# Two-block transformer step: adaptive shift and scale by PE products, division after the weighted sum, gate work one expert pair earlier

## The chip, the cores and the metric
One NeuronCore of one Trainium2 chip runs the whole program. The metric is device microseconds of one execution. TensorE (PE), VectorE (DVE), ScalarE (ACT) and GpSimd (POOL) each run their own instructions in order; SyncE (SP) issues most transfers, ACT and POOL a few.

## The reference, cut to what matters
```python
def first_block(x, c, ...):
    c_act = jax.nn.silu(c)
    mod = c_act @ ada_w[l] + ada_b[l]
    sh_a, sc_a, gt_a, sh_m, sc_m, gt_m = [m[:, None, :] for m in jnp.split(mod, 6, axis=-1)]
    h = rmsnorm(x, norm_mix_g[l]) * (1.0 + sc_a) + sh_a
    proj = h @ w_in[l]                      # four mixers of 4 heads
    x = x + gt_a * (mixed @ w_out[l])
    h = rmsnorm(x, norm_ffn_g[l]) * (1.0 + sc_m) + sh_m
    x = x + gt_m * conv_ffn(h, ...)

def forgetting_attention(...):              # one of the four mixers
    s = q @ k * scale + (cq[..., :, None] - cum[..., None, :])
    p = jax.nn.softmax(jnp.where(dist >= 0, s, NEG), axis=-1)
    return p @ v

def second_block(x, p, ...):
    x = x + jnp.concatenate([y_pool, y_attn], axis=-1) @ w_out[i]
    x = x + expert_choice_ffn(rms_norm(x, norm_ffn[i]), ...)      # 16 experts
    g = jax.nn.sigmoid(rms_norm(x, norm_ple[i]) @ w_ple_gate[i])
    e = rms_norm(p[i] @ w_ple_proj[i], norm_ple_post[i])
    x = x + g * e
```
x is 512 tokens of 1024 features in float32, c one vector of 1024. An expert has 1024 x 2048 gate and up weights and 2048 x 1024 down weights and takes 64 tokens. Subtracting the query's own term cq from a row of scores does not change that row's softmax, and dividing a row of exponentials by its sum can be done before or after the product with v.

## The kernel before, in words
Activations of the first block and of the second block's attention lie with features on the partitions: eight blocks of 128 features by 512 tokens. A product in float32 precision is made of three fp32r products (`mm3`, lines 331 to 334) of a high and a low half; `weights_` (lines 318 to 326) splits a weight panel on ACT (`whi`) and DVE (`wlo`). A scheduler orders the instructions of each engine from the program and its priorities; on the chip each engine keeps that order.

**Start (lines 264 to 504).** x is loaded in four pieces, then the shift and scale columns of ada_w, transposed, as eight 1 MB tiles `adr` in a ring of four (`ada_load`, line 299). `bd` and `tb2` (lines 458, 461) are a round trip through memory that makes the bias table; the products `pf` (line 511) reverse it with the matrix `flip`, a part of `cst` that line 505 loads. The eight squares of x are summed, `rstd_rows` and `to_features` make the reciprocal root `rr` for each token, and x is multiplied by it (line 481, half on DVE and half on POOL). For each feature block k, DVE reduces the shift's half of `adr` against c (line 485), POOL multiplies the scale's half (line 490) and ACT sums it (line 491); DVE makes `shf` and `amul`, and ACT and DVE make `hTh` and `hTl` (lines 495 to 497). The first three projections (`early`) run along, block by block.

**Mixers (to line 1050).** Four mixers in two halves each run two at a time as generators; `run` mixes them with the projections that come next. `ada_more` (line 348) computes the other four vectors of mod out of 64 tiles `adw` of 256 KB with two buffers: POOL multiplies a tile by its element of c (line 355) and adds it to `ada_a` (line 360); after eight tiles four PE products `pm` sum over partitions. 48 of the tiles come during the mixers. `fox` (line 851) is the forgetting attention: for each of four query blocks and two heads, `fb` is the key's cumulative gate less the query's (line 861) plus the causal mask (line 862); `softmax_part` (line 613) adds it to the scores and takes the exponential, `scale_parts` (line 638) divides both heads' exponentials by their sums `l` (lines 639 and 643), then they are transposed and multiplied by v. `na` (line 1184), in the second block, has the same steps for eight heads, two at a time.

**Experts (line 1060 to the end).** Experts come in pairs. A pair reads 48 chunks of 1 MB (`chunk`, line 1294), each used by eight products with 64 output rows, the two experts' products side by side in PE's two column halves (lines 1697, 1698, 1727, 1728). Chunks lie in rings of buffers: 2 `x16`, 5 `chy`, 6 `chr`, 3 `chl`. `chl` is used for chunks until pair E_AT, `chr` until pair RETIRE; then they hold the embedding (`pe`), the gate's weights and its sums. Between the steps of a pair, `between` gives PACE turns to a list of other work: `spread` (an expert's output onto the tokens), `embedding`, `gate_base` (the gate's products `pg` of one block of 128 tokens, started in the pairs that BASE names) and `gate_pair` (the products `z` of a pair's own output with the gate's weights, and their scatter `po` onto the blocks whose base is done).

Of the kernel before, what the change touches and what calls it, by code (L numbers as in the profile page):

```python
# [9 lines left out]
FT = mybir.dt.float32  # L10
# [9 lines left out]
D = 1024  # L20
# [6 lines left out]
SCV = []  # L27
# [3 lines left out]
PACE = [1.0, 1.0, 1.0, 1.0, 2.2, 2.2, 2.2, 2.2]  # L31
# [5 lines left out]
RETIRE = 4  # L37
BASE = {4: [0], 5: [1], 6: [2], 7: [3]}
E_AT = 2
# [79 lines left out]
def prep(i):  # L119
# [33 lines left out]
    o["c"] = i["c"].reshape(1, D)  # L153
# [5 lines left out]
    aw = i["ada_w"][0][:, :2 * D].T.reshape(2, 8, 128, D)  # L159
    o["adaT"] = np.ascontiguousarray(aw.transpose(1, 2, 0, 3)).reshape(8, 128, 2 * D)  # L160
# [70 lines left out]
def _build(ctx, tc, nc, a, dbg, stop):  # L231
# [35 lines left out]
    cact = su.tile([128, D], FT, name="cact")  # L267
    A.dma_start(cact, bcast(a["c"], D))
# [30 lines left out]
    def ada_load(n):  # L299
        for j in range(n):  # L300
            t = su.tile([128, 2 * D], FT, name="adr", tag="adr", bufs=4)
            SY.dma_start(t, a["adaT"][len(ada_raw)])
            ada_raw.append(t)
# [45 lines left out]
    def ada_more(n):  # L349

        for m in range(ada_next[0], min(64, ada_next[0] + n)):
            w = tmp[0].tile([128, 512], FT, name="adw", tag="adw", bufs=2)
            SY.dma_start(w, a["ada2"][m])
            k = m % 8
            P.tensor_tensor(w, w, cT[:, k:k + 1].to_broadcast([128, 512]), op=OP.mult)  # L355
            if k == 0:
                ada_next[1] = tmp[0].tile([128, 512], FT, name="ada_a", tag="ada_a", bufs=1)
                P.tensor_copy(ada_next[1], w)
            else:
                P.tensor_tensor(ada_next[1], ada_next[1], w, op=OP.add)  # L360
            if k == 7:
                pm = ps("pm", "dense", 2)
                for j in range(4):
                    T.matmul(pm[:, j:j + 1], ada_next[1][:, 128 * j:128 * j + 128], K["ones"], start=True, stop=True)
                c_ = slice(16 + m // 8 * 4, 20 + m // 8 * 4)
                V.tensor_tensor(mod[:, c_], pm[:, 0:4], C["ada_b"][:, c_], op=OP.add)
            ada_next[0] = m + 1

    def rstd_of(acc, scale, out, n=128):

        v, y = sm([128, 8], "rv")[0:n, 0:out.shape[-1]], sm([128, 8], "ry")[0:n, 0:out.shape[-1]]
        V.tensor_scalar(v, acc, scale, EPS, op0=OP.mult, op1=OP.add)
        A.activation(y, v, AF.Ln)
        A.activation(y, y, AF.Exp, scale=-0.5)
        V.scalar_tensor_tensor(v, v, -0.5, y, op0=OP.mult, op1=OP.mult)
        V.tensor_tensor(v, v, y, op=OP.mult)
        V.scalar_tensor_tensor(out, v, 1.5, y, op0=OP.add, op1=OP.mult)

    def rstd_rows(sq, ind, n, scale, tag="dense"):

        ms = ps("ms", tag, 2)
        for t in range(4):
            T.matmul(ms[:, n * t:n * t + n], sq[:, 128 * t:128 * t + 128], ind, start=True, stop=True)
        y = sm([128, 16], "rs")[:, 0:4 * n]
        for c in range(0, 4 * n, 8):
            rstd_of(ms[:, c:min(c + 8, 4 * n)], scale, y[:, c:min(c + 8, 4 * n)])
        return y
# [64 lines left out]
    for k in range(8):  # L452
        ada_load(1)
        for e in range(2) if k == 0 else range(k + 1, k + 2):
            if e < EARLY:
                raws.append(panel(a["w_in"][e]))
        if k == 0:
            SY.dma_start(bd, bv)
        if k == TBK:
            for j in range(4):  # L460
                SY.dma_start(tb2[:, j].rearrange("p (h c) -> p h c", h=2),
                             bass.AP(tensor=bd.tensor, offset=bd.offset + 768 * j, ap=[[1, 128], [384, 2], [1, 256]]))
    sq = []
# [15 lines left out]
    shf = cp.tile([128, 8], FT, name="shf")  # L479
    for k in range(8):  # L480
        (V if k < XV else P).tensor_tensor(xin[:, k], xin[:, k], rr, op=OP.mult)
    for k in range(8):
        c_ = slice(k, k + 1)
        w = ada_raw[k]
        V.scalar_tensor_tensor(w[:, 0:D], w[:, 0:D], 1.0, cact, op0=OP.mult, op1=OP.mult, accum_out=mod[:, c_])
        sc = mod[:, 8 + k:9 + k]
        if k in SCV:
            V.scalar_tensor_tensor(w[:, D:], w[:, D:], 1.0, cact, op0=OP.mult, op1=OP.mult, accum_out=sc)
        else:
            P.tensor_tensor(w[:, D:], w[:, D:], cact, op=OP.mult)  # L490
# [153 lines left out]

    def pv(acc_, v, p_, i, sizes, start, stop):
# [78 lines left out]
    cqc = pa.tile([128, 16], FT, name="cqc")  # L724

    def gates_and_decay():
# [14 lines left out]
        V.tensor_copy(t[0:4], cum)  # L741
# [6 lines left out]
        V.tensor_copy(cqc.rearrange("p (t c) -> p t c", t=4), pg[:, :, 0:4])  # L748
# [102 lines left out]
    def fox(hp):  # L851
        q, kk, v, ckb = st["fox", hp]
        o = ps("od", "o", 2)
        for i in range(4):
            nk = 128 * (i + 1)
            l = sm([128, 2], "l2")
            e = []
            for par in range(2):
                h = 2 * hp + par
                fb = t2k("fb")  # L860
                V.tensor_scalar(fb[:, :nk], ckb[:, par, :nk], cqc[:, 4 * i + h:4 * i + h + 1], None, op0=OP.subtract)
                V.tensor_tensor(fb[:, nk - 128:nk], fb[:, nk - 128:nk], K["cm"], op=OP.add)
# [8 lines left out]
        A.activation(mix[:, 2 + hp], o, AF.Copy)  # L871
# [312 lines left out]
    def na(hp):  # L1184
        q, kk, v, nb = st["na", hp]
        o = ps("od", "o", 2)
        for b in range(4):
            nk = 248 if b else 256
            l = sm([128, 2], "l2")
            e = []  # L1190
            for par in range(2):
# [14 lines left out]
        m, o = mix2[:, 4 + hp].rearrange("p (r c) -> p c r", r=8), o.rearrange("p (c r) -> p c r", r=8)  # L1206
# [593 lines left out]
```

## Time and profile before
| what | value |
|---|---|
| median of 3 runs | 2106.22 us (2103.95 to 2110.03) |
| the profiled execution | 2106.01 us |
| its span, first to last instruction | 2104.2 us |
| mean granted TensorE clock | 0.972 of full speed |
| busy: PE, DVE, ACT, POOL | 1904.4, 851.3, 555.5, 243.8 us |
| moved by transfers | 523.67 MB |

Busy is the time in which an engine executes, stage by stage with different limits, so the shares of the whole span say little about any one stage. The page, the windows by stage, the chain of waits and the timeline are views of one execution. Ends of PE's products are modelled; what one product costs PE is read from the distance of starts.

### The profile page before, as it was taken

What the parts mean: (1) busy time and instruction counts of PE and PEld (TensorE: products, weight loads), DVE (VectorE), ACT (ScalarE), POOL (GpSimd) and SP (SyncE); (2) the same over time, 40 slices, a digit from 0 to 9 for tenths busy, and PEclk for the clock granted to TensorE, in tenths of its full rate; (3) what the DMA queues carried; (4) which work ended last, traced back from release to release, by engine and by line L of the source; (5) the groups of instructions that cost most, each with busy time, mean ns of one, the idle gap of its engine ahead of it and who ended that gap; (6) DMA issues with size and microseconds to landing.
All of it is one profiled execution on the core that took longest, in us unless ns stands there. A gap on an engine that the chain in (4) does not pass through costs nothing.

```text
span 2104.2 us, 22827 instructions
## 1 busy us (share of the span) xinstructions
PE 1904.4 (91%) x8822; PEld 1067.6 (51%) x8822; DVE 851.3 (40%) x1761; ACT 555.5 (26%) x1089; POOL 243.8 (12%) x211
## 2 busy tenths in 40 slices
PE   2898988979999999999989988988779999999997
PEld 1566656658888887777643322322223333333343
DVE  7887887875444335677441101210010020110114
ACT  4655544534323324445310000200000000100012
POOL 5540333350200000000100000000030000000001
PEclk9998998989999999999989999999989999999998
DMA  6532223333322223222589999899999999999991
GB/s 245 167 116 66 86 81 93 108 101 105 112 107 92 100 91 100 76 79 77 237 357 421 422 422 420 368 420 419 421 419 395 420 385 367 418 390 396 401 387 68
DMA packets 95084, 523.67 MB, mean 249 GB/s; under 512 B 11405, under 2 KB 12853, under 8 KB 44032
## 3 DMA queue, kind: packets, MB, share of 16 engines
q1 hardware_dynamic: 89936, 501.53, 60.9%
q0 software_dynamic: 3552, 17.82, 2.3%
q10 hardware_dynamic: 1488, 2.87, 0.4%
q8 instruction: 69, 1.13, 0.2%
q14 instruction: 39, 0.32, 0.0%
HBM read 510.83 MB, written 4.27 MB: 245 GB/s over the span
## 4 chain that ended last, share of the span: by engine, by line
PE 67%; DMA 18%; DVE 10%; ACT 2%; issue 2%; POOL 0%; SPq 0%; DVEq 0%; POOLq 0%; ACTq 0%
DMA ch<-in_w_ue_dram 8%; DMA ch<-in_w_de_dram 6%; PE ua L1697 5%; PE ga L1697 4%; PE ga L1698 4%; PE yd L1728 4%; PE yd L1727 3%; PE pg L1553 3%; PE z L1553 2%; PE ag L332 2%; PE ag L333 2%; PE ag L334 2%; PE od L649 2%; PE av L332 2%; PE av L333 2%; PE av L334 2%
## 5 line engine op out<-in xcount | busy, mean ns | idle before, releaser
L1697 PE MATMUL ga<-ch,xe 128*64 128x512 f32 x512 | 242.5, 610 | 9.0 <-DMA ch<-in_w_ge_dram 9.0
L1698 PE MATMUL ua<-ch,xe 128*64 128x512 f32 x512 | 231.1, 596 | 21.4 <-DMA ch<-in_w_ue_dram 21.4
L1728 PE MATMUL yd<-ch,hts 128*64 128x512 f32 (+1 forms) x544 | 233.5, 576 | 16.4 <-DMA ch<-in_w_de_dram 16.3
L1698 PE MATMUL ga<-ch,xe 128*64 128x512 f32 x512 | 236.5, 607 | 5.4 <-DMA ch<-in_w_ge_dram 5.4
L1727 PE MATMUL yd<-ch,hts 128*64 128x512 f32 (+1 forms) x544 | 234.8, 576 | 0.0
L1697 PE MATMUL ua<-ch,xe 128*64 128x512 f32 x512 | 233.5, 596 | 0.0
L325 DVE TENSOR_TENSOR wlo<-pan,whi 128x1024 fp32r<-128x1024 f32 x119 | 156.1, 1312 | 159.2 <-ACT whi L322 154.0
L322 ACT ACTIVATE whi<-pan 128x1024 fp32r<-128x1024 f32 x119 | 125.9, 1058 | 212.9 <-PE ag L333 93.8
L1708 DVE TENSOR_TENSOR sg<-sg,ua 128x512 f32<-128x512 f32 x32 | 22.0, 686 | 265.4 <-PE ua L1698 265.4
L1728 PEld LDWEIGHTS yd<-ch,hts 128*64 128x64 f32 x544 | 72.2, 138 | 110.4 <-issue 75.4
L1698 PEld LDWEIGHTS ga<-ch,xe 128*64 128x64 f32 x512 | 67.2, 139 | 93.3 <-issue 78.5
L1698 PEld LDWEIGHTS ua<-ch,xe 128*64 128x64 f32 x512 | 67.4, 137 | 88.7 <-issue 52.3
L1697 PEld LDWEIGHTS ua<-ch,xe 128*64 128x64 f32 x512 | 67.0, 137 | 77.0 <-issue 74.6
L338 DVE TENSOR_TENSOR ys<-yg,ys 128x512 fp32r<-128x512 f32 (+1 forms) x17 | 12.5, 733 | 229.9 <-ACT ys L337 229.9
L1697 PEld LDWEIGHTS ga<-ch,xe 128*64 128x64 f32 x512 | 66.0, 139 | 66.1 <-issue 54.0
L1727 PEld LDWEIGHTS yd<-ch,hts 128*64 128x64 f32 x544 | 71.6, 138 | 50.3 <-issue 47.9
L1687 ACT ACTIVATE hts<-pth 128x512 f32<-128x512 f32 x32 | 19.1, 596 | 266.9 <-PE pth L1686 266.9
L1731 ACT ACTIVATE yg<-yd,gs 128x512 f32<-128x512 f32 (+1 forms) x17 | 11.3, 662 | 287.2 <-PE yd L1728 196.3
L355 POOL TENSOR_TENSOR adw<-adw,cT 128x512 f32<-128x512 f32 x64 | 77.7, 1215 | 40.5 <-DMA adw<-in_ada_dram 40.3
L360 POOL TENSOR_TENSOR ada_a<-ada_a,adw 128x512 f32<-128x512 f32 x56 | 78.3, 1399 | 4.4
L1707 ACT ACTIVATE sg<-ga 128x512 f32<-128x512 f32 x32 | 19.1, 597 | 224.0 <-PE ga L1698 224.0
L618 ACT ACTIVATE e<-e,m 128x256 f32<-128x256 f32 (+8 forms) x128 | 65.1, 509 | 49.4 <-DVE m L616 46.9
(896 smaller groups left out, 3833.8 us busy)
## 6 DMA issues: line engine op xcount, KB each, us to landing
ch<-in_w_de_dram SPq DMA_DIRECT2D x128, 1024.0 KB, 13.7
ch<-in_w_ue_dram SPq DMA_DIRECT2D x125, 1024.0 KB, 9.9
ch<-in_w_ge_dram SPq DMA_DIRECT2D x120, 1024.0 KB, 13.4
pan<-in_w_up_dram SPq DMA_DIRECT2D x44, 512.0 KB, 3.2
adw<-in_ada_dram SPq DMA_DIRECT2D x64, 256.0 KB, 2.6
pan<-in_w_in_dram SPq DMA_DIRECT2D x24, 512.0 KB, 3.7
pan<-in_w_dn_dram SPq DMA_DIRECT2D x22, 512.0 KB, 3.2
adr<-in_adaT_dram SPq DMA_DIRECT2D x8, 1024.0 KB, 9.2
```

The source lines that it names most:

```text
L322: A.activation(hi, raw, AF.Copy)
L325: eng.tensor_tensor(lo, raw, hi.bitcast(FT), op=OP.subtract)
L332: T.matmul(out, wh, xh, start=first, stop=False)
L333: T.matmul(out, wh, xl, start=False, stop=False)
L334: T.matmul(out, wl, xh, start=False, stop=last)
L355: P.tensor_tensor(w, w, cT[:, k:k + 1].to_broadcast([128, 512]), op=OP.mult)
L360: P.tensor_tensor(ada_next[1], ada_next[1], w, op=OP.add)
L1553: T.matmul(out[c_], w[:, c_], x_, start=start, stop=stop)
L1697: T.matmul(acc_[m][0:64], xe[:, kk, 0:64], wa[:, k], start=kk == 0, stop=kk == 7)
L1698: mm = T.matmul(acc_[m][64:128], xe[:, kk, 64:128], wb[:, k], start=kk == 0, stop=kk == 7)
L1727: T.matmul(yd[0:64], hts[:, kk, 0:64], wa[:, k_], start=kk == 0, stop=kk == 15)
L1728: mm = T.matmul(yd[64:128], hts[:, kk, 64:128], wb[:, k_], start=kk == 0, stop=kk == 15)
```

## The change
Shift and scale of the first norm: `ada1` holds columns of ada_w as they are. For each feature block PE multiplies eight 128-row blocks of it with the eight columns of silu(c), each repeated over 32 columns, into four groups of 32 output rows; ACT copies the row out, and two products with the vector `four` bring shift and scale back to columns. x is no longer multiplied by `rr` ahead; `make_h` does it with the scale on DVE. Loads `bd` and `tb2` go through POOL's queue. `ada_more` multiplies on ACT. `rstd_of` takes up to 16 columns at once. `fox` leaves out the query's term, adds the mask in place from the last block back, and divides after the product with v (`divided`), as `na` does. E_AT, RETIRE, BASE and PACE move the embedding and the gate one pair earlier.

```diff
-PACE = [1.0, 1.0, 1.0, 1.0, 2.2, 2.2, 2.2, 2.2]
+PACE = [1.0, 1.0, 1.0, 2.2, 2.2, 2.2, 2.2, 1.5]
-RETIRE = 4
-BASE = {4: [0], 5: [1], 6: [2], 7: [3]}
-E_AT = 2
+RETIRE = 3
+BASE = {3: [0], 4: [1], 5: [2], 6: [3]}
+E_AT = 1
...
-            P.tensor_tensor(w, w, cT[:, k:k + 1].to_broadcast([128, 512]), op=OP.mult)
             if k == 0:
                 ada_next[1] = tmp[0].tile([128, 512], FT, name="ada_a", tag="ada_a", bufs=1)
-                P.tensor_copy(ada_next[1], w)
+                A.activation(ada_next[1], w, AF.Copy, scale=cT[:, 0:1])
             else:
+                A.activation(w, w, AF.Copy, scale=cT[:, k:k + 1])
                 P.tensor_tensor(ada_next[1], ada_next[1], w, op=OP.add)
...
-            SY.dma_start(bd, bv)
+            P.dma_start(bd, bv)
...
-                SY.dma_start(tb2[:, j].rearrange("p (h c) -> p h c", h=2),
+                P.dma_start(tb2[:, j].rearrange("p (h c) -> p h c", h=2),
...
+    four = su.tile([128, 1], FT, name="four")
+    V.memset(four, 0.0)
+    for i in range(4):
+        V.memset(four[32 * i:32 * i + 1], 1.0)
     for k in range(8):
-        (V if k < XV else P).tensor_tensor(xin[:, k], xin[:, k], rr, op=OP.mult)
+        with tc.high_priority(offset=400):
+            pr_ = ps("pr", "=s", 2)
+            for i in range(8):
+                q = 32 * (i % 4)
+                T.matmul(pr_[q:q + 32, 0:256], cT[:, i:i + 1].to_broadcast([128, 32]), ada_raw[k][:, i], start=i < 4,
+                         stop=i >= 4)
+            row = su.tile([128, 256], FT, name="row", tag="row", bufs=2)
+            A.activation(row, pr_[:, 0:256], AF.Copy)
+            for i in range(2):
+                T.matmul(pr_[:, 256 + i:257 + i], row[:, 128 * i:128 * i + 128], four, start=True, stop=True)
+            V.tensor_tensor(shf[:, k:k + 1], pr_[:, 256:257], C["ada_b"][:, k:k + 1], op=OP.add)
+            V.tensor_scalar(amul[:, k:k + 1], pr_[:, 257:258], scb[:, k:k + 1], C["g_mix"][:, k:k + 1], op0=OP.add,
+                            op1=OP.mult)
     for k in range(8):
         c_ = slice(k, k + 1)
-        w = ada_raw[k]
-        V.scalar_tensor_tensor(w[:, 0:D], w[:, 0:D], 1.0, cact, op0=OP.mult, op1=OP.mult, accum_out=mod[:, c_])
...
-            P.tensor_tensor(w[:, D:], w[:, D:], cact, op=OP.mult)
-            A.activation(w[:, D:], w[:, D:], AF.Copy, accum_out=sc)
...
+        last = make_h(xin[:, k], rr, k, amul[:, c_], shf[:, c_])
...
+    def divided(o, l, out):
+
+        A.activation(out, o, AF.Copy)
+        r = sm([128, 8], "r8", 2)
+        V.reciprocal(r, l)
+        V.tensor_tensor(out, out, to_features(r, 2), op=OP.mult)
...
-        for i in range(4):
+        for i in (3, 2, 1, 0):
             nk = 128 * (i + 1)
...
+            V.tensor_tensor(ckb[:, :, nk - 128:nk], ckb[:, :, nk - 128:nk], K["cm"].unsqueeze(1).to_broadcast([128, 2, 128]),
+                            op=OP.add)
             for par in range(2):
-                h = 2 * hp + par
-                fb = t2k("fb")
-                V.tensor_scalar(fb[:, :nk], ckb[:, par, :nk], cqc[:, 4 * i + h:4 * i + h + 1], None, op0=OP.subtract)
-                V.tensor_tensor(fb[:, nk - 128:nk], fb[:, nk - 128:nk], K["cm"], op=OP.add)
...
-            scale_parts(e, l, nk)
...
-        A.activation(mix[:, 2 + hp], o, AF.Copy)
+        divided(o, ls_.rearrange("p i h -> p (i h)"), mix[:, 2 + hp])
```

PE's order at the start, before; `rb` spreads the reciprocal root over the tokens, acc_ are the early projections:
```order
L397 MATMUL rb<-cst,rs 128x128 x4
L332 MATMUL acc__208<-hTh,whi 128x512
L332 MATMUL acc__216<-hTh,whi 128x512
L332 MATMUL acc__239<-hTh,whi 128x512
L333 MATMUL acc__208<-hTl,whi 128x512
```
and with the change:
```order
L483 MATMUL pr<-adr,cT 32x256 x8
L379 MATMUL ms<-cst,sq 128x1 x4
L488 MATMUL pr<-four,row 128x1 x2
L392 MATMUL rb<-cst,rs 128x128 x4
L508 MATMUL pf<-tb_109,cst 128x512
L483 MATMUL pr<-adr,cT 32x256 x8
L508 MATMUL pf<-tb_109,cst 128x512
L488 MATMUL pr<-four,row 128x1 x2
L328 MATMUL acc__318<-hTh,whi 128x512
```
Two reversing products `pf`, which stood behind the early projections, now stand ahead of the second column block's eight products and of the first projection.

POOL's order at the first modulation tiles, before:
```order
L355 TENSOR_TENSOR adw<-adw,cT 128x512 x2
L358 COPY ada_a<-adw 128x512
L360 TENSOR_TENSOR ada_a<-ada_a,adw 128x512
L355 TENSOR_TENSOR adw<-adw,cT 128x512
L360 TENSOR_TENSOR ada_a<-ada_a,adw 128x512
```
and ACT's with the change, in a stretch of the first mixers (`e` are the exponentials, `pts` evacuates their transposes, `kt` belongs to the compressed keys):
```order
L615 ACTIVATE e,l_1040<-e,m 128x256
L318 ACTIVATE whi<-pan 128x1024
L355 ACTIVATE adw<-adw,cT 128x512 x2
L615 ACTIVATE e,l_1068<-e,m 128x256 x2
L355 ACTIVATE adw<-adw,cT 128x512 x2
L629 ACTIVATE pts<-pt 128x256
L318 ACTIVATE whi<-pan 128x1024
L615 ACTIVATE e,l_1096<-e,m 128x384 x2
L355 ACTIVATE adw<-adw,cT 128x512 x2
L615 ACTIVATE e,l_1187<-e,m 128x384 x2
L766 ACTIVATE kt,st<-kc 31x64
L355 ACTIVATE adw<-adw,cT 128x512
```
The multiplication of each tile has moved from POOL into ACT's order, in places two at a time between exponentials.

## Rows read from the trace of the kernel before
**Rows 1.** The page: the chain that ended last, by engine.
```profile
PE 67%; DMA 18%; DVE 10%; ACT 2%; issue 2%; POOL 0%; SPq 0%; DVEq 0%; POOLq 0%; ACTq 0%
```
**Rows 2.** Windows by stage: length, busy us of PE, PEld, DVE, ACT, POOL; PEclk, DMA, GB/s.
```profile
0.00:67.00 67.00, 27.22 (x87) 17.62 (x88) 50.14 (x71) 33.75 (x53) 34.59 (x24) 1.00 0.66 244
67.00:460.00 393.00, 345.50 (x1846) 249.13 (x1844) 318.80 (x790) 197.06 (x481) 139.98 (x111) 0.95 0.31 98
...
846.00:1003.00 157.00, 154.72 (x796) 117.86 (x795) 110.87 (x295) 72.21 (x169) 1.61 (x3) 0.98 0.25 78
...
1418.00:1547.00 129.00, 96.25 (x424) 32.07 (x421) 12.08 (x16) 9.77 (x15) 9.66 (x7) 0.98 1.01 420
...
1677.00:1811.00 134.00, 130.75 (x575) 45.92 (x573) 16.66 (x28) 10.62 (x17) 1.31 (x3) 0.97 0.96 386
...
1941.00:2089.00 148.00, 147.92 (x709) 61.50 (x706) 28.73 (x54) 22.34 (x50) 0.19 (x1) 1.00 0.76 305
```
**Rows 3.** The start: timeline rows (start, us, what), transfers (KB, us to landing).
```profile
1.97 0.54 POOL L438 DMA_DIRECT2D rel<-in_rel_dram  x1
...
11.20 0.55 DVE L445 COPY bv<-pb 8x384 f32<-8x384 f32 x1 [1.60 <-PE pb L443]
...
66.97 0.40 PE L333 MATMUL acc__239<-hTl,whi 128*128 128x512 f32 x1
...
67.21 0.40 PE L334 MATMUL acc__239<-hTh,wlo 128*128 128x512 f32 x1
...
cst<-in_cst_dram POOLq DMA_DIRECT2D x1, 329.5 KB, 6.3
...
adw<-in_ada_dram SPq DMA_DIRECT2D x64, 256.0 KB, 2.6
```
**Rows 4.** PE's timeline: small products, a product 32 wide, a change of shape.
```profile
17.80 1.87 PE L383 MATMUL ms<-cst,sq 128*128 128x1 f32 x8 [6.63 <-DVE sq L474]
...
1022.36 1.05 PE L1312 MATMUL lg<-x,wrt 128*32 128x512 f32 x2
...
1970.08 0.59 PE L1697 MATMUL ga<-ch,xe 128*64 128x512 f32 x1
...
1970.50 0.59 PE L1697 MATMUL ga<-ch,xe 128*64 128x512 f32 x1
1970.51 0.59 PE L1698 MATMUL ga<-ch,xe 128*64 128x512 f32 x1
1971.03 0.72 PE L1537 MATMUL po<-zs,ott 128*128 128x512 f32 x2
1971.69 0.64 PE L1697 MATMUL ua<-ch,xe 128*64 128x512 f32 x1
```
**Rows 5.** Window sums (POOL busy, POOL quiet); tiles adw and wlo: ns min/median/max; idle us, times.
```profile
sum 120.00, PE 93.88 PEld 66.38 DVE 108.03 ACT 43.88 POOL 101.00; mean PE 7.82 PEld 5.53 DVE 9.00 ACT 3.66 POOL 8.42
...
sum 120.00, PE 116.34 PEld 86.14 DVE 93.85 ACT 73.47 POOL 4.27; mean PE 9.70 PEld 7.18 DVE 7.82 ACT 6.12 POOL 0.36
...
L355 POOL TENSOR_TENSOR adw<-adw,cT x64: 1031/1052/2025, 67.0 to 579.1; 128x512 f32<-128x512 f32 x64
L360 POOL TENSOR_TENSOR ada_a<-ada_a,adw x56: 1261/1292/2150, 70.7 to 580.9; 128x512 f32<-128x512 f32 x56
...
  DMA adw<-in_ada_dram: 40.3, 30
...
L325 DVE TENSOR_TENSOR wlo<-pan,whi x119: 1202/1226/3356, 21.9 to 1031.1; 128x1024 fp32r<-128x1024 f32 x119
```
**Rows 6.** Groups of instructions, 67 to 460 us: busy us, mean ns | idle before.
```profile
L643 DVE TENSOR_SCALAR e<-e,r 128x128 f32<-128x128 f32 (+7 forms) x64 | 32.9, 550 | 0.6
...
L861 DVE TENSOR_SCALAR fb<-ckb,cqc 128x128 f32<-128x128 f32 (+3 forms) x16 | 9.0, 560 | 0.0
...
L862 DVE TENSOR_TENSOR fb<-fb,cst 128x128 f32<-128x128 f32 x16 | 8.4, 526 | 0.3
```
**Rows 7.** Tile z in the whole run: count, ns min/median/max, first and last start.
```profile
L1553 PE MATMUL z<-ch,yt x256: 592/592/644, 1658.0 to 2086.0; 128*64 128x512 f32 x128
```

More of the change, by code (lines that the diff above doesn't have):

```diff
@@ L158, in prep @@
     o["xT"] = np.ascontiguousarray(i["x"][0].T.reshape(8, 128, S).transpose(1, 0, 2))
-    aw = i["ada_w"][0][:, :2 * D].T.reshape(2, 8, 128, D)
-    o["adaT"] = np.ascontiguousarray(aw.transpose(1, 2, 0, 3)).reshape(8, 128, 2 * D)
+    aw = i["ada_w"][0][:, :2 * D].reshape(8, 128, 2, 8, 128)
+    o["ada1"] = np.ascontiguousarray(aw.transpose(3, 1, 0, 2, 4)).reshape(8, 128, 2 * D)
     aw = i["ada_w"][0][:, 2 * D:].reshape(8, 128, 8, 512)
@@ L297, in _build, with ada_load @@
     ada_raw = []
[L299 to L303, printed above, removed]
+    def ada_load():
+        t = su.tile([128, 2 * D], FT, name="adr", tag="adr", bufs=4)
+        SY.dma_start(t, a["ada1"][len(ada_raw)])
+        ada_raw.append(t.rearrange("p (k c) -> p k c", k=8))
     wn = [0, 0]
@@ L369, in rstd_of @@
     def rstd_of(acc, scale, out, n=128):
-        v, y = sm([128, 8], "rv")[0:n, 0:out.shape[-1]], sm([128, 8], "ry")[0:n, 0:out.shape[-1]]
+        v, y = [sm([128, 16], n_, 4)[0:n, 0:out.shape[-1]] for n_ in ("rv", "ry")]
         V.tensor_scalar(v, acc, scale, EPS, op0=OP.mult, op1=OP.add)
@@ L384, in rstd_rows @@
         y = sm([128, 16], "rs")[:, 0:4 * n]
-        for c in range(0, 4 * n, 8):
-            rstd_of(ms[:, c:min(c + 8, 4 * n)], scale, y[:, c:min(c + 8, 4 * n)])
+        rstd_of(ms[:, 0:4 * n], scale, y)
         return y
@@ L430, in make_h @@
         A.activation(oh, t, AF.Identity, bias=sh)
-        V.scalar_tensor_tensor(ol, t, sh, oh.bitcast(FT), op0=OP.add, op1=OP.subtract)
+        return V.scalar_tensor_tensor(ol, t, sh, oh.bitcast(FT), op0=OP.add, op1=OP.subtract)
     rel = su.tile([33, 8], FT, name="rel")
@@ L452, in _build @@
     for k in range(8):
-        ada_load(1)
+        ada_load()
         for e in range(2) if k == 0 else range(k + 1, k + 2):
@@ L1186, in na @@
         o = ps("od", "o", 2)
+        l = sm([128, 4, 2], "l8", 2)
         for b in range(4):
             nk = 248 if b else 256
-            l = sm([128, 2], "l2")
             e = []
@@ L1198, in na @@
                     T.matmul(s[:, :nk], q[:, par, 128 * b:128 * b + 128], k_, start=x_ == 0, stop=x_ == 1)
-                e.append(softmax_part(s, nb[:, par, 0:248] if b else nb[:, par, 248:], nk, l[:, par:par + 1]))
+                e.append(softmax_part(s, nb[:, par, 0:248] if b else nb[:, par, 248:], nk, l[:, b, par:par + 1]))
             yield
-            scale_parts(e, l, nk)
             pts = [transpose_p(e[par], nk, par) for par in range(2)]
@@ L1205, in na @@
             yield
-        m, o = mix2[:, 4 + hp].rearrange("p (r c) -> p c r", r=8), o.rearrange("p (c r) -> p c r", r=8)
+        t = p2k("on")
+        divided(o, l.rearrange("p i h -> p (i h)"), t)
+        m, o = mix2[:, 4 + hp].rearrange("p (r c) -> p c r", r=8), t.rearrange("p (c r) -> p c r", r=8)
         A.activation(m[:, 0:56], o[:, 8:], AF.Copy)
```

22 lines of the change are left out of this document (2 added, 20 removed).

## The prediction
> **What bounds the kernel now.** I read the page first, then the stages, then the rows inside the three stages that the change touches. The chain that ended last belongs for two thirds to PE and for 18% to transfers [rows 1], which is a mean over stages with different limits. By stage [rows 2] the reader is to see four cases. In the first 67 us PE works 27.2 us and DVE 50.1: the start waits for DVE. In the mixers (67 to 460) PE is busy 345.5 of 393 us, with DVE at 318.8. In the second block's attention (846 to 1003) PE is busy 154.7 of 157. Among the experts, pair 3 (1418 to 1547) has DMA at 1.01 and PE at 96 of 129, so transfers bound it, while pair 5 (1677 to 1811) has PE at 130.8 of 134 and pair 7 with its tail (1941 to 2089) at 147.9 of 148: there PE is the bound.
>
> The profiled execution took 2106.01 us, 1.8 more than its span and 0.2 under the median of 2106.22. I sum against 2106.0. About 0.3%, 6.3 us, is what a measurement of this kernel can tell from no change.
>
> **The start.** Removed are, for each of eight feature blocks, two reductions over 128x1024: one of DVE, one of POOL and ACT; PE waited for what they gave. The last early product starts at 67.21, one spacing (0.24) after the one before it, and is through at 67.4 [rows 3]. Afterwards the shift and scale come from PE, and PE's own order decides. It puts the first flip product (pf) ahead of the second column block. That product waits for tb2 and the flip table, which now both come through POOL's queue: bv is ready at 11.75; the store of bd lands, like the small adw loads, after some 2.6; four tb2 issues of 0.54 and then the table's 6.3 give 22.8, and 23 is taken [rows 3].
>
> From there I add PE's rows. A set of eight 32-column products is not in the trace. One of 512 columns, 32 wide and alone, takes 1.05 with its end [rows 4], so 256 columns some 0.45: eight one after another cost 3.6. Two 64-wide products side by side share 0.42, the spacing of the ga rows [rows 4]; by pairs the eight cost 1.8, by fours 0.9. I take 1.4, between pairs, which the trace shows, and fours, which it doesn't. A change of shape and back costs 0.3 (po starts 0.53 after ga instead of 0.42, ua 0.66 after two po of 0.24) [rows 4]. The two products with `four` cost 0.94, half of the four ms products' 1.87 [rows 4]. Nine projection products of 0.23, a little under the spacing of the last two, are 2.05. A feature block thus takes 1.4 + 0.3 + 0.94 + 2.05 = 4.7. Two pf products (0.9 each), the second column block with its switch (1.7) and its `four` products (0.94) put the first projection product at 27.4; seven periods and one last block end at 62.4. **Start: -5**, from -8 (0.9 a set) to +11 (3.6 a set). DVE needs under 2 us per block for xn, hTl and the two columns, so it is covered by PE's 4.7; at 420 GB/s a 1 MB column block lands every 2.5 us, covered too.
>
> The Trainium skill, TensorEngine Tiling (Array Packing), Theoretical Speedup, gives up to four times for a side of 32 or less; no run here shows four abreast. By that rule a set costs 0.9 and the start gains 8 instead of 5.
>
> **The mixers.** First POOL. I set two times twelve slices of 10 us against each other: where POOL is busiest (from 70, 80, 130, 140, 220, 230, 270, 320, 330, 390, 440 and 450 us) it worked 101 of 120 us and PE 93.9; where it is quiet (from 100, 110, 120, 190, 200, 210, 240, 250, 300, 350, 360 and 410) it worked 4.3 and PE 116.3 [rows 5]. So PE idles 26.1 against 3.7. DVE is the link: the same split of a panel takes 1.2 us or up to 3.4 [rows 5]. The change takes the 64 multiplications (1.05 at the median) off POOL and leaves the 56 additions of 1.29: 47% of that work goes. 47% of the excess idle of 22.4 is **-11**.
>
> Then DVE's own work. In the forgetting heads fb costs 9.0 + 8.4, and 16 of the 64 scalings by 1/l, at 0.55, 8.8 [rows 6]; eight wider mask additions (some 3) and, twice, a broadcast copy and a product over 128x512 come back, some 2 together. DVE is relieved of about 21 us. As PE is 97% busy wherever POOL is quiet, most of it was covered: I take **-8**, with 0 and -21 as ends. ACT gets 48 multiplications of about 0.6 in this stage, 29 us on an engine that idles 196 of 393; I charge **+1**. The single chain of small operations for the differential heads, instead of two, I count as nothing, covered by PE. The mixers give **-18**, from -4 to -36.
>
> **Second attention.** The same deferred division takes 32 scalings off DVE and puts 16 transposes on PE, which is full there; at no more than the 0.24 of a projection product each, 4 us are added. The softmax steps lose their waits for the scalings, which can't be worth more than the 2.3 us that PE idles plus what DVE's lateness hides in its rows. **-1**, from -3 to +4. The first block's ffn keeps its products and PE's full stretch: 0.
>
> **The experts.** The gate's base products, its pairwise products and the embedding all move one pair earlier. z has 256 records in four pairs, two abreast each 0.43: 13.8 us a pair [rows 7]; the base products pg are as many. Pair 7 loses a base and gains about 4 us of scatters; pair 3 gains a base and a z: 96 + 27.6 = 124, under the 129 that its transfers took. But the four gate weights, 10 us of transfers, now come before pair 3 instead of before pair 4, and one z more is computed in all. Starting pair 3 at 1428: 124, then 131, 132, 132 for pairs 4 to 6 (pair 5 of before with some scatters more or less), and 148 - 13.8 + 4 = 138 for pair 7: the tail starts at 2085 instead of 2089. Against it, from pair 3 on only 7 of the 13 weight buffers are left, and with 7 the transfers ran at 386 GB/s in pair 5 [rows 2] instead of 420. **-2**, from -15 to +10.
>
> Sum: -5 - 18 - 1 - 2 = -26, **2080**.
>
> **Rivals.**
> (a) *ACT is held by the modulation loads; slower.* ACT now executes the multiplication, in order, and stands where the load has not landed. POOL waited 40.3 us for these loads, 30 times [rows 5], 2.6 us from issue to landing [rows 3], and little queued behind it; behind ACT stand the exponentials and evacuations. The order puts two or three blocks close together with two buffers. If ACT stood a whole load in each of 48 blocks, 125 us, it would be occupied for 197 + 29 + 125 = 351 of 393 us and pass PE's 345: the mixers' gain would go and some 25 would be added, **2123**. It decides from 0.54 us on the path per block (26/48). Against it: while POOL was busy ACT worked only 43.9 of 120 us [rows 5].
> (b) *The 32-wide products run one after another.* Start +11 instead of -5: **2096**.
> (c) *The first flip product comes late.* All of PE stands behind it in order; if each of the six issues on POOL's queue is held for one DVE operation of 1.2 us, the first projection slips 7: **2087**. The Trainium skill, SBUF — State Buffer, SBUF: two separate sides, says that a transfer issued from the GpSimd queue starves for its descriptors while DVE holds the shared port; this row-based price is what that would do here.
> (d) *PE is the floor of the mixers*, so only -4 there: **2094**.
> (e) *The mixers give all that DVE is relieved of*, -36: **2062**.
> (f) *The experts' last pair pays in full*, -15: **2067**.
> (g) *The moved multiplications change nothing*, because POOL's additions stretch to fill the same slices and stall DVE as before: the mixers lose 11 of their 18, **2091**.
>
> **Chances.** Forecast 0.40 (2071 to 2089). (a) 0.07, (b) 0.08, (c) 0.08, (d) 0.10, (e) 0.10, (f) 0.10, (g) 0.07. The range 2056 to 2099 takes in (b) to (g) and leaves out (a) and sums of rivals on one side. Slower by over 0.3%: 0.07, from (a). Within 0.3%: 0.06, where (b) meets (d) or (g). Faster by over 0.3%: 0.87.
>
> **What would show it.** Start: the last early product near 62 us, DVE no longer above 90% before it, the eight-product sets at 1.0 to 1.8 us, pf waiting for the cst transfer near 23. Mixers: shorter by some 18, POOL's busy time there about halved, panel splits seldom over 1.3, PE busy over 91% of the stage. Experts: PE fuller in pair 3, pair 7 shorter, the total hardly moved. Wrong if ACT's idle time is ended by adw transfers for tens of us, if PE waits at pr or pf after 30 us, or if pairs 1 to 3 grow by more than pair 7 loses.

## The result, and the profile after

The changed kernel takes 2082.05 us (median of 4 runs, 2080.72 to 2084.36); the kernel before took 2107.67 beside it. The ratio is 0.9881, with a 95% interval of [0.9863, 0.9899]. The forecast was 2080. The profiled execution took 2082.38 us, with a span of 2080.6.

Both traces can be cut at the same five places of the program: the last early product, the last output product of the first block, the first ffn product, the first product of the second attention, the first product of the experts.

| stage | before | after | difference | forecast |
|---|---|---|---|---|
| start | 67.2 | 64.5 | -2.7 | -5 |
| mixers | 386.8 | 364.4 | -22.4 | -18, with part of the pause |
| pause before the ffn | 14.2 | 9.1 | -5.1 | (in the mixers) |
| ffn | 366.1 | 366.8 | +0.7 | 0 |
| second attention and routing | 236.1 | 236.0 | -0.1 | -1 |
| experts to the end | 1033.8 | 1039.8 | +6.0 | -2 |
| span | 2104.2 | 2080.6 | -23.6 | -26 |

The chain that ended last, on the page of the changed kernel, answers to [rows 1]:
```profile
PE 72%; DMA 14%; DVE 6%; ACT 3%; issue 2%; POOL 1%; ACTq 0%; POOLq 0%; DVEq 0%; SPq 0%
```
DVE's share of the chain fell from 10% to 6%, PE's rose from 67% to 72%.

Windows of the changed kernel: start, mixers, pause, then pairs 1, 2 and 3 and the last pair with its tail (columns as in [rows 2]):
```profile
0.00:64.50 64.50, 41.14 (x251) 24.47 (x252) 26.21 (x65) 24.48 (x40) 9.37 (x17) 1.00 0.68 257
64.50:428.90 364.40, 340.25 (x1849) 252.97 (x1847) 274.92 (x725) 224.17 (x524) 67.14 (x50) 0.94 0.34 104
428.90:438.00 9.10, 2.56 (x15) 1.73 (x13) 5.35 (x11) 3.67 (x8) 0.00 (x0) 0.74 0.25 92
...
1143.90:1269.20 125.30, 113.97 (x493) 37.95 (x489) 23.43 (x38) 16.82 (x33) 1.85 (x3) 0.96 0.95 394
1269.20:1411.30 142.10, 114.03 (x479) 38.67 (x477) 17.63 (x27) 11.99 (x18) 16.92 (x13) 0.96 1.01 420
1411.30:1532.70 121.40, 103.55 (x474) 36.44 (x473) 6.21 (x10) 6.09 (x10) 0.00 (x0) 1.00 0.96 392
1927.90:2066.00 138.10, 136.87 (x640) 56.31 (x640) 29.58 (x55) 21.43 (x50) 0.44 (x1) 1.00 0.80 328
```
The same cuts in the kernel before (mixers, pause, pairs 1 and 2; pair 3 and the tail are in [rows 2]):
```profile
67.20:454.00 386.80, 344.93 (x1845) 248.96 (x1843) 313.36 (x785) 194.66 (x478) 133.94 (x108) 0.95 0.31 97
454.00:468.20 14.20, 3.31 (x14) 2.49 (x12) 9.01 (x13) 3.96 (x8) 10.79 (x8) 0.66 0.44 148
...
1173.40:1285.90 112.50, 97.43 (x430) 33.51 (x426) 12.29 (x21) 8.62 (x14) 1.91 (x4) 0.98 1.01 421
1285.90:1418.00 132.10, 113.56 (x489) 38.29 (x490) 23.40 (x38) 16.65 (x33) 1.31 (x3) 0.99 0.97 399
```
In the mixers PE's work nearly stayed where it was, 345 and 340 us; most of what went is the rest of the stage: PE was not busy for 41.9 us of it before and for 24.2 after. POOL's busy time halved, as forecast, and DVE's fell by 38 us. Among the experts pairs 1 and 2 got 12.8 and 10.0 us longer.

POOL's and PE's timeline rows at the start of the changed kernel:
```profile
16.27 2.94 POOL L456 DMA_DIRECT2D tb<-bd  x4 [5.01 <-DMA bd<-bv]
19.20 0.57 POOL L502 DMA_DIRECT2D cst<-in_cst_dram  x1
...
29.95 2.05 PE L508 MATMUL pf<-tb,cst 128*128 128x512 f32 x2 [9.35 <-DMA cst<-in_cst_dram]
31.93 1.93 PE L483 MATMUL pr<-adr,cT 128*32 128x256 f32 x16
35.20 0.48 PE L328 MATMUL acc__318<-hTh,whi 128*128 128x512 f32 x1
38.06 1.07 PE L483 MATMUL pr<-adr,cT 128*32 128x256 f32 x16
41.57 1.07 PE L483 MATMUL pr<-adr,cT 128*32 128x256 f32 x16
61.68 0.51 PE L328 MATMUL acc__318<-hTh,whi 128*128 128x512 f32 x1 [0.54 <-ACT hTh L425]
64.50 0.40 PE L330 MATMUL acc__344<-hTh,wlo 128*128 128x512 f32 x1
```
Its transfers up to 40 us (how busy the 16 DMA engines were, in tenths of each microsecond; then KB and median us to landing):
```profile
DMA  0269999999999999999999999999700000449900
...
tb<-bd POOLq DMA_DIRECT2D x4, 256.0 KB, 9.0
cst<-in_cst_dram POOLq DMA_DIRECT2D x1, 329.5 KB, 10.7
```
The stretch in which the flip table (`cst`) was under way, here and then in the kernel before (columns as in [rows 2]):
```profile
19.20:29.90 10.70, 1.12 (x4) 0.72 (x4) 1.74 (x4) 1.32 (x2) 0.57 (x2) 1.00 0.91 356
...
56.60:62.90 6.30, 5.04 (x19) 3.36 (x20) 4.94 (x12) 4.98 (x8) 0.62 (x2) 1.00 0.93 369
```
PE stood 9.35 us for the flip table, which landed at 29.9 and not at 23. Behind that a feature block took 3.9 us (the sets come at 41.57, 45.48, 49.38), and not 4.7: a set of eight products, two records each, is through in 1.07. The second set, behind the wait and a `pf`, took 1.93, though the granted clock of the whole start is 1.00 in the windows; why was not tried.

### The profile page after: what moved, and what is told of

Read it like the earlier page. It is cut to its first block, busy times and chain, and to the rows that moved or that the text cites. A ratio compares the mean times of both kernels' runs of the same rounds, so it can differ in the third digit from the quotient of the medians.

```text
span 2080.6 us, 23361 instructions
## 1 busy us (share of the span) xinstructions
PE 1933.5 (93%) x9094; PEld 1087.5 (52%) x9094; DVE 787.0 (38%) x1670; ACT 583.3 (28%) x1134; POOL 132.3 (6%) x132
## 4 chain that ended last, share of the span: by engine, by line
PE 72%; DMA 14%; DVE 6%; ACT 3%; issue 2%; POOL 1%; ACTq 0%; POOLq 0%; DVEq 0%; SPq 0%
DMA ch<-in_w_ue_dram 6%; PE ua L1698 6%; PE ga L1699 5%; PE ga L1698 5%; PE yd L1728 4%; DMA ch<-in_w_de_dram 4%; PE yd L1729 3%; PE z L1554 3%; PE pg L1554 2%; PE od L653 2%; PE ag L328 2%; PE ag L329 2%; PE ag L330 2%; PE av L328 2%; PE av L329 2%
## 5 line engine op out<-in xcount | busy, mean ns | idle before, releaser
L1699 PE MATMUL ua<-ch,xe 128*64 128x512 f32 x512 | 231.2, 595 | 17.7 <-DMA ch<-in_w_ue_dram 17.5
L321 DVE TENSOR_TENSOR wlo<-pan,whi 128x1024 fp32r<-128x1024 f32 x119 | 149.0, 1252 | 163.1 <-ACT whi L318 161.2
L1698 PEld LDWEIGHTS ua<-ch,xe 128*64 128x64 f32 x512 | 67.2, 137 | 90.7 <-issue 88.5
L1554 PE MATMUL z<-ch,yt 128*64 128x512 f32 x320 | 90.5, 594 | 1.3 <-DVE yt L1739 1.3
## 6 DMA issues: line engine op xcount, KB each, us to landing
ch<-in_w_ue_dram SPq DMA_DIRECT2D x125, 1024.0 KB, 10.5
```

What stands on the lines that cost most here:

```text
L321: eng.tensor_tensor(lo, raw, hi.bitcast(FT), op=OP.subtract)
L1554: T.matmul(out[c_], w[:, c_], x_, start=start, stop=stop)
L1698: T.matmul(acc_[m][0:64], xe[:, kk, 0:64], wa[:, k], start=kk == 0, stop=kk == 7)
L1699: mm = T.matmul(acc_[m][64:128], xe[:, kk, 64:128], wb[:, k], start=kk == 0, stop=kk == 7)
```

## Experiments

Twelve kernels, in three groups. The first four are the changed kernel with one part undone each, timed beside the kernel before.

### POOL multiplies again
```diff
-                A.activation(ada_next[1], w, AF.Copy, scale=cT[:, 0:1])
-                A.activation(w, w, AF.Copy, scale=cT[:, k:k + 1])
+            P.tensor_tensor(w, w, cT[:, k:k + 1].to_broadcast([128, 512]), op=OP.mult)
+                P.tensor_copy(ada_next[1], w)
```


> The changed kernel with one part undone: POOL multiplies the modulation tiles again. In the changed kernel the stretch from the last early product to the first ffn product is 27.5 us shorter, and POOL works 67 us in it instead of 145. Theory: the 64 multiplications on POOL stretched DVE's operations, so putting them back costs the forecast's 11 us in the mixers and the 5 us by which the pause before the ffn became shorter: 2098 (2092 to 2103), with that pause back at 13 to 14 us. Rival: POOL's additions stretch DVE as before and the multiplications don't matter: 2081 to 2085. Second rival: ACT's 0.71 us each cost as much as POOL's stretching did, then undoing it is worth nothing or a gain: under 2081.

Measured: 2106.59 us, 0.9997 of before [0.9981, 1.0013]. All but 1 us of the change is gone, more than the theory's range allowed. Windows of this kernel, the mixers and then five stretches inside them:
```profile
65.50:451.20 385.70, 351.38 (x1849) 258.24 (x1847) 297.05 (x724) 192.42 (x467) 138.69 (x110) 0.92 0.31 95
...
265.00:270.00 5.00, 5.00 (x24) 2.79 (x22) 4.97 (x15) 3.01 (x11) 2.72 (x3) 1.00 0.41 131
270.00:275.00 5.00, 3.46 (x16) 1.79 (x16) 4.96 (x9) 2.71 (x7) 4.58 (x5) 0.82 0.38 134
275.00:280.00 5.00, 4.23 (x15) 3.08 (x14) 4.65 (x9) 0.99 (x4) 4.66 (x4) 0.50 0.63 150
280.00:285.00 5.00, 4.08 (x13) 3.10 (x12) 3.93 (x8) 1.42 (x4) 3.26 (x3) 0.66 0.38 112
285.00:290.00 5.00, 4.04 (x26) 2.52 (x27) 4.47 (x12) 2.37 (x7) 2.50 (x3) 1.00 0.19 52
```
DVE runs the same instructions as in the changed kernel (724 and 725), yet is busy 297.1 us instead of 274.9. PE is idle 34.3 us instead of 24.2, and what it does takes 11 us longer at a clock of 0.92 instead of 0.94. The five stretches show both halves: while POOL and DVE are busy together DVE falls behind and PE idles (270 to 275), and then PE runs at the lower of its two levels, 1.2 GHz (0.50, from 275 to 280), until after 280. In this place what DVE's lateness costs PE is paid twice. It is one place of one execution.

### Division and query's term as before
```diff
-        divided(o, ls_.rearrange("p i h -> p (i h)"), mix[:, 2 + hp])
+            scale_parts(e, l, nk)
+        A.activation(mix[:, 2 + hp], o, AF.Copy)
...
+                V.tensor_scalar(fb[:, :nk], ckb[:, par, :nk], cqc[:, 4 * i + h:4 * i + h + 1], None, op0=OP.subtract)
+                V.tensor_tensor(fb[:, nk - 128:nk], fb[:, nk - 128:nk], K["cm"], op=OP.add)
```


> The changed kernel with one part undone: the forgetting heads and the second block's attention divide before the product with v again, and the query's term is back. Theory of the forecast: DVE's 21 us in the mixers were mostly covered by PE, so this costs 8 us there and about 1 in the second attention: 2091 (2086 to 2096). Rival: DVE held PE all the way, and all 21 us come back: 2103 or more. Rival: wholly covered, and with the broadcasts for the division gone a little is gained: 2079 to 2083.

Measured: 2084.35 us, 0.9906 [0.9878, 0.9934]: 2.3 by the medians, within the scatter, near the last rival and far from the theory. Windows of this kernel, mixers and pause:
```profile
64.10:426.30 362.20, 332.76 (x1840) 246.89 (x1839) 277.46 (x768) 222.08 (x520) 64.20 (x48) 0.96 0.34 102
426.30:439.40 13.10, 3.40 (x15) 2.53 (x13) 7.71 (x13) 5.96 (x11) 2.54 (x2) 0.61 0.39 138
```
The groups of `fb` in it, on DVE (busy us, mean ns | idle before):
```profile
L858 DVE TENSOR_SCALAR fb<-ckb,cqc 128x128 f32<-128x128 f32 (+3 forms) x16 | 7.7, 481 | 0.0
L859 DVE TENSOR_TENSOR fb<-fb,cst 128x128 f32<-128x128 f32 x16 | 4.6, 289 | 0.3
```
The mixers are not longer. The pause is, 13.1 us instead of 9.1, with two of POOL's additions in it; mixers and pause together take 375.3 us instead of 373.5. And the work itself was smaller than it looked before: `fb` took 7.7 + 4.6 us here, 9.0 + 8.4 in [rows 6], where POOL multiplied beside it.

### Experts' schedule as before
```diff
-PACE = [1.0, 1.0, 1.0, 2.2, 2.2, 2.2, 2.2, 1.5]
-RETIRE = 3
-BASE = {3: [0], 4: [1], 5: [2], 6: [3]}
-E_AT = 1
+PACE = [1.0, 1.0, 1.0, 1.0, 2.2, 2.2, 2.2, 2.2]
+RETIRE = 4
+BASE = {4: [0], 5: [1], 6: [2], 7: [3]}
+E_AT = 2
```


> The changed kernel with one part undone: E_AT, RETIRE, BASE and PACE as before. In the changed kernel the experts take 6.0 us longer than before (1039.8 against 1033.8): pairs 1 and 2 together 22.9 longer, the last pair 10.2 shorter. Theory: this is the schedule's own doing, so undoing it gives 2076 (2073 to 2079), with pair 1 near 112 and pair 2 near 132. Rival, the forecast's: the schedule gains 2 and what was lost comes from elsewhere (weights that arrived earlier or later because the stages ahead are shorter): 2082 to 2085.

Measured: 2078.27 us, 0.9867 [0.9842, 0.9891], 3.8 less than the changed kernel. The experts take 1033.2 us of its profiled execution, pairs 1 and 2 112.7 and 131.9. The new schedule is a loss, and by itself, as the theory had it.

### Start as before
The edit puts back the column blocks as `adaT`, the reductions on DVE, POOL and ACT, and the multiplication of x by the root.

> The changed kernel with one part undone: shift and scale of the first norm by DVE, POOL and ACT again, x multiplied by the root first, bd and tb2 on SP's queue. In the changed kernel the last early product starts 2.7 us earlier and the next panel's first 4.5. Theory: the start is worth 3 to 5: 2086 (2084 to 2088). Rival: its gain is eaten behind it, since the next panels wait for weights or bias anyway: 2081 to 2083. If the four parts stand by themselves, the four differences to the changed kernel sum to about 25.6, the whole change; if parts overlap, they sum to less.

Measured: 2083.68 us, 0.9897 [0.987, 0.9923]: 1.6 by the medians, between the ranges of theory and rival and within the scatter, the last early product at 67.4. Together the four parts give 24.5 + 2.3 - 3.8 + 1.6 = 24.6 of the 25.6 us, so no overlap shows: the multiplication is nearly all of it.

### The additions left out, and the additions on DVE
In the first kernel the addition covers 1x8 elements, on DVE; in the second DVE does multiplication and addition in one instruction:
```diff
-                P.tensor_tensor(ada_next[1], ada_next[1], w, op=OP.add)
+                V.tensor_tensor(ada_next[1][0:1, 0:8], ada_next[1][0:1, 0:8], w[0:1, 0:8], op=OP.add)
```
```diff
-                A.activation(w, w, AF.Copy, scale=cT[:, k:k + 1])
-                P.tensor_tensor(ada_next[1], ada_next[1], w, op=OP.add)
+                V.scalar_tensor_tensor(ada_next[1], w, cT[:, k:k + 1], ada_next[1], op0=OP.mult, op1=OP.add)
```


> Cost of what POOL still does, measured by leaving it out: of the additions that sum the modulation tiles, 128x512 on POOL, only 1x8 elements are added, on DVE, so seven eighths of the sums that make the modulation are left out. With the multiplication back on POOL the mixers were 21 us longer and DVE's stretching beside POOL 23 us more, about one for one; in the changed kernel 29 us of stretching beside POOL are left in the mixers. Theory (stretched DVE operations stand on PE's path one for one): the 29 us less the small additions (56 of 0.17, 10 us) go, bounded by the 24 us that PE idles in the mixers: 2065 (2058 to 2070). Rival: what PE still idles there has other causes, and the additions lie beside work: 2078 to 2083.

> POOL out of the modulation altogether: one DVE instruction multiplies a tile by its element of c and adds it to the sum. DVE gets 56 operations of about 0.74 (41 us in the whole run, 36 in the mixers), loses 29 us of stretching there; ACT loses 0.71 for each. Theory (a stretched DVE operation costs because POOL's come in lumps behind one another; work of DVE's own is mostly covered, as the 21 us of divisions were, whose return cost 2): the mixers shorten by about 10: 2072 (2066 to 2078). Rival: DVE's time counts the same whether stretched or worked: 36 - 29 = +7: 2089. Rival: nothing, 2080 to 2084.

Measured: without the additions 2065.64 us, 0.9815 [0.9763, 0.9867]; with them on DVE 2079.57, 0.9861 [0.9815, 0.9906]. The mixers of the first and then of the second:
```profile
64.40:408.50 344.10, 329.68 (x1848) 246.12 (x1847) 251.70 (x772) 222.68 (x522) 0.55 (x1) 0.97 0.35 109
```
```profile
64.50:426.80 362.30, 341.15 (x1848) 254.13 (x1847) 275.79 (x772) 195.94 (x474) 0.56 (x1) 0.94 0.33 103
```
The additions that stay on POOL cost most of that again: 16.4 us by the medians, 20 us of mixers in the profiled execution, which is the fastest of four (2060.07 to 2074.80 us) and has half of the 20 from PE's shorter busy time at a clock of 0.97 instead of 0.94. But they can't be had by giving them to DVE. Its 56 instructions of 0.746 us bring its busy time back to 275.8, what it was with POOL's stretching, and the mixers to 362. That is the last rival, no difference within the scatter: these runs don't tell whether DVE's time in those places is stretching or its own work.

### The reversing products late
`mm3` returns its last product, and the four `pf` are queued on PE behind the last projection product of the second-last feature block (second-last of eight, and not sixth-last as the expectation says):
```diff
+                mid = end if k <= 6 else mid
...
-        T.matmul(pf, K["flip"], tb2[:, j], start=True, stop=True)
+        with tc.issue_after(mid.ins):
+            T.matmul(pf, K["flip"], tb2[:, j], start=True, stop=True)
```


> The changed kernel with the four reversing products queued on PE behind the sixth-last projection block of the start instead of two of them ahead of the first projection. In the changed kernel PE stands 9.35 us at the first of them, until the flip table lands at 29.9. Theory: the first projection starts at about 25 instead of 35.2, the periods of 3.9 us follow, and the last early product comes 7 to 9 us earlier: 2074 (2072 to 2077). Rival: the column blocks or panels land too late for that (eight of 1 MB in a ring of four), PE waits for them instead: 2079 to 2083. Rival: the bias table is late for the first mixers: 2082 or more.

Measured: 2071.52 us, 0.9827 [0.9781, 0.9872], 10.5 less than the changed kernel. PE's timeline in this kernel: the second set, the first projection, the last early product, and the last two `pf`:
```profile
20.32 1.94 PE L483 MATMUL pr<-adr,cT 128*32 128x256 f32 x16
23.63 0.78 PE L328 MATMUL acc__318<-hTh,whi 128*128 128x512 f32 x1
...
54.90 0.40 PE L330 MATMUL acc__344<-hTh,wlo 128*128 128x512 f32 x1
55.13 1.88 PE L510 MATMUL pf<-tb,cst 128*128 128x512 f32 x4
```
The wait is gone and the whole program behind it comes 9.6 us earlier. The column blocks keep up.

### The embedding in pair 2, the gate early
```diff
-E_AT = 1
+E_AT = 2
```


> The changed kernel with the embedding in pair 2 as before, the gate still one pair earlier than before. Theory: pair 1 returns from 125 to 112.5; pair 2, bound by transfers, carries both the embedding's and the gate's loads, 142 plus the 5 us of the embedding's at most, pairs 3 to 7 as in the changed kernel: experts shorter by 6 to 12, 2073 (2069 to 2077). Rival: what pair 1 gains pair 2 or 3 loses, since the bytes ahead of pair 3 are the same: 2080 to 2084. Rival: the embedding's products, now beside the gate's, hold up the gate's first base: over 2086.

Measured: 2080.83 us, 0.9863 [0.9815, 0.991], not to be told from the changed kernel. Pairs 1 and 2 of this kernel:
```profile
1153.40:1265.90 112.50, 97.54 (x429) 33.55 (x425) 12.30 (x21) 8.64 (x14) 1.91 (x4) 0.98 1.01 421
1265.90:1419.40 153.50, 128.74 (x541) 43.77 (x542) 27.70 (x44) 20.29 (x38) 16.92 (x13) 0.97 0.97 402
```
112.5 + 153.5 = 266.0 against 125.3 + 142.1 = 267.4: pair 2 takes what pair 1 gives, the first rival. So the 23 us that pairs 1 and 2 lost to the kernel before (244.6) are not the embedding's; they belong to the gate's three settings, RETIRE, BASE and PACE, which were not tried one by one.

### The multiplication alone, and what beats both kernels
The kernel before with nothing but ACT's multiplication; the changed kernel with `pf` late and the old schedule (called best); and best with one more edit each, from above.

> The kernel before with one part of the change alone: ACT multiplies the modulation tiles. Undoing this part in the changed kernel gave back 24.5 of the 25.6 us, half as PE's idle time and half as time at the lower granted clock. Theory: this part alone makes nearly the whole change, 2083 (2079 to 2088), the mixers 365 us from the last early product to the last output product instead of 387. Rival: in the kernel before, where DVE also divides and subtracts the query's term, DVE stays late without POOL's multiplications, and only the forecast's 11 to 16 come: 2090 to 2096.

> The changed kernel with two things put right: the reversing products late (alone it gave 2071.5, the start 9.6 us shorter), and E_AT, RETIRE, BASE and PACE as before (alone 2078.3, experts 6 shorter). Theory: start and experts share nothing, so both gains stand: 2066 to 2068 (2062 to 2071). Rival: with the experts 10 us earlier the first weights are less far ahead and pair 0 waits: 2071 or more.

> The kernel of the run best, and DVE multiplies and adds the modulation tiles in one instruction, so that POOL and ACT do none of it. In the changed kernel this gave 2079.6 instead of 2082, within the scatter. Theory: DVE's own 36 us in the mixers cost about what POOL's stretching and ACT's 40 us cost: within 3 us of best. Rival: ACT and POOL free are worth the 7 us by which PE's idle time there was shorter without POOL's additions: best less 5 to 8. Rival: DVE's work counts: best plus 5 to 8.

> The kernel of the run best, with division and query's term of the forgetting heads and the second attention as in the kernel before. Theory of the forecast: 8 us in the mixers and 1 in the second attention come back: best plus 7 to 11. Rival (undone in the changed kernel it cost 2.3 by the medians, 5 by the ratios, unresolved): DVE's 21 us there were covered by PE: best plus 0 to 4.

| kernel | us | ratio to before |
|---|---|---|
| multiplication alone | 2080.14 | 0.9872 [0.9854, 0.989] |
| best | 2064.34 | 0.9794 [0.9779, 0.981] |
| best, additions on DVE | 2064.04 | 0.9791 [0.9774, 0.9809] |
| best, division as before | 2065.71 | 0.9806 [0.9787, 0.9825] |

Mixers and pause of the kernel with the multiplication alone:
```profile
67.20:429.90 362.70, 337.68 (x1845) 249.69 (x1843) 275.63 (x785) 226.65 (x532) 65.77 (x48) 0.95 0.34 104
429.90:443.20 13.30, 3.31 (x15) 2.50 (x13) 8.02 (x13) 5.83 (x11) 2.66 (x2) 0.67 0.42 136
```
This one edit makes the kernel before 27.8 us faster, no less than the whole change does. Best is 43.6 faster than before: the two repairs add up (17.7 us together, 10.5 and 3.8 one by one). The division is worth 1.4 us in it, and the additions on DVE 0.3, both within the scatter, as the rival of the first and the theory of the second had it.

## Why the forecast held, and which of its terms did not

The time came out 2 us from the forecast. The terms did not come out as well: the mixers with the pause give 27.5 us where 18 were taken, the experts lose 6 where 2 were to be gained, the start gives half, and inside the mixers two errors offset each other. That the sum is near is partly luck.

**POOL: "47% of the excess idle of 22.4 is -11".** This term was sized at half. The multiplication alone, put into the kernel before, shortens the mixers by 24.1 us (386.8 to 362.7), and undone in the changed kernel it lengthens them by 21.3. The twelve busy slices hold 101 us of POOL's work, and the mixers 134, so the excess should have been scaled up by a third, to 29.7 us, of which 47% are 14. That is about what went of PE's idle time: 16.9 us where the multiplication alone is moved (41.9 to 25.0), 10.1 where it is undone. PE's busy time for the same products was not in the sum, and it differs too, by 7 and by 11 us. How much of this is the granted clock the traces leave open: undone, the mixers ran at 0.92 instead of 0.94, but alone the window shows 0.95 with it and without. Over all runs the mean granted clock was 0.9696 before and 0.9738 in the changed kernel; (1 - clock) x span is 64 us before and 54.5 after, so up to 9.5 of the whole 25.6 us can be this. In the mixers of the two profiled executions it shows nothing: 0.05 x 386.8 and 0.06 x 364.4 are 19 and 22 us.

The Trainium skill, SBUF — State Buffer, SBUF: two separate sides, says that a GpSimd instruction that reads SBUF and a DVE instruction with two inputs in SBUF exclude each other for the whole instruction, and that ACT waits for nobody. The rows agree on both: with POOL's multiplications back, DVE's same 724 instructions cost 22 us more, while ACT's multiplication took between 0.704 and 0.727 us each time in the changed kernel, beside POOL or not.

**DVE: "I take -8, with 0 and -21 as ends".** The end 0 was right. With the division moved and with it back, mixers and pause together take 373.5 and 375.3 us; in best 377.1 and 377.0. The term also counted twice: part of the 17.4 us of `fb` in [rows 6] was POOL's stretching, already paid for in the term before. (The stage's ends, -4 and -36, are not sums of the terms, which would give -10 and -31.)

**The pause before the ffn** stood in the forecast's stage as if it were mixers. It is 4 to 5 us shorter where no modulation tile is left in it: POOL was busy 10.8 us in it before and not at all after, and in the kernels with the old division, the multiplication alone among them, two or three additions stay in it and it takes 13.1 to 13.3 us. Where the last tiles fall in the order was not foreseen. It moves time between mixers and pause as well: with the old division the mixers are shorter by 2 to 4.

**The start: -5.** The first projection was taken too early (27.4, it is 35.2) and the seven periods behind it too long (32.9, they take 26.5, from 35.20 to 61.68): two errors that nearly offset. A period is 3.9 us instead of 4.7, and the sum counts seven sets behind the first projection where six are left. A set of eight takes 1.07 us instead of 1.4, the two `four` products 0.50 instead of 0.94. Eight one after another were worked out at 3.6, so by that estimate four abreast make it 3.4 times faster. The Trainium skill, TensorEngine Tiling (Array Packing), Theoretical Speedup, gives up to four times; by that rule the set (0.9) would have come nearer, the start (-8) would not. Rival (c), a late flip product, came true at its price of 7 us, in three pieces: the store of `bd` took 5.2 us to land instead of 2.6, the four issues of `tb2` 2.94 instead of 2.16, and the table 10.7 instead of 6.3. Its mechanism, POOL's queue held by DVE's work, does not fit the last piece: DVE was busy 1.74 of the 10.7 us, and 4.94 of the 6.3 in the kernel before. Nor does the share of the DMA engines tell the two apart, 0.91 and 0.93. What made the table late stays open; in both kernels it landed as the transfers under way ran out (at 28 to 30 us here, at 62 to 63 there). A landing time read in one place of the program was no price for another.

**ACT held by the loads, rival (a),** did not come: ACT waited 10.0 us for tiles, 11 times, in the mixers. Over the run it was 17.1 us, and in the kernel with the multiplication alone 21.8, which was still 27.8 us faster than before.

**The experts: -2.** Pairs 4 to 7 came as forecast: the last pair with its tail takes 138.1 us (138), pair 3 121.4 (124). What failed is "Starting pair 3 at 1428", that is, 10 us for pairs 1 and 2. They lose 23, of which pair 3 gives back 8 (129.5 to 121.4). The gate's four weights were priced by their own 4.2 MB. But pair 3 of before, in which they landed, took 129 us [rows 2], and pair 1, with as much work on PE (97.4 and 96.3 us), 112.5: the price was some 17, and could have been read from two rows. Length times rate of the windows says what it is made of: that pair 3 moved 54 MB and that pair 1 47, and pairs 1 and 2 move 109 MB in the changed kernel instead of 100, which is 21 us at 420 GB/s; pair 3 then moves 48. In pair 2 of the changed kernel there is one more step behind the loads, in POOL's timeline:
```profile
1388.74 3.74 POOL L1566 TENSOR_TENSOR ch<-ch,cols 128x1024 f32<-128x1024 f32 x2 [117.83 <-DMA ch<-in_w_pg_dram]
1392.64 1.27 POOL L1478 DMA_INDIRECT xg<-xd,at  x1 [0.16 <-issue]
1393.93 3.75 POOL L1566 TENSOR_TENSOR ch<-ch,cols 128x1024 f32<-128x1024 f32 x2
1401.58 0.42 POOL L1484 COPY gs<-xg 64x1 f32<-64x1 f32 x2 [3.90 <-DMA xg<-xd,at]
1402.08 7.44 POOL L1566 TENSOR_TENSOR ch<-ch,cols 128x1024 f32<-128x1024 f32 x4
```
POOL multiplies the gate's weights by the norm's factors for 15 us, and stands 3.9 us in between for the next pair's gather. The gate's first products start at 1398.6, before pair 3 begins, and PE waits for POOL's step 9.4 us in six pieces; in the kernel before, where POOL was through at 1553 and the first of these products started at 1574.7, it did not wait for it at all. The transfers ran on at 419 GB/s meanwhile, so how much of the 23 us this step makes is open; it was not tried.

## What to carry to other kernels

Where two engines stretch each other, don't price the work that moves by its own duration or by its share of one bin: run the same instructions of the engine that is held through both traces, and take the excess as the most that the bound can give: 37.7 us less on DVE gave 24.1 us of mixers (the multiplication alone), 22.2 more cost 21.3 (undone). Put a product that needs a small, late transfer behind work that is ready: all of an in-order engine waits with it. And a stage bound by transfers takes as long as everything that it moves: price a transfer that changes its place by the rows of the stage where it lands, not by its own bytes.

## What the runs showed of the hardware that was not expected

The granted clock goes with PE's waits, and with the time: in kernels with POOL's multiplication the mean granted clock over the runs was 0.969 to 0.970, without it 0.973 to 0.975. Most of the scatter goes with it as well: the kernel with the embedding in pair 2 ranges from 2074.39 to 2088.11 us, at clocks of 0.979 to 0.972, and its profiled execution, at 0.972, took 372.9 us for the mixers that the changed kernel did in 364.4, with PE idle 24.9 and 24.2 us.

The same 330 KB took 6.3 and 10.7 us to land while the 16 DMA engines were equally busy (0.93 and 0.91), and the same eight products 1.93 us just behind a wait and 1.07 in a full stretch, at a granted clock of 1.00 in both.
